# Two-layer chunked attention and retention trunk: value products a round later, column parts, later sines, side work spread by a running debt, logit scale inside the minimum

## The chip, the core and the metric

The kernel runs on one core of one Trainium2 chip. A core has a matrix engine (TensorE, PE in the profile; PEld is its weight load), a vector engine (VectorE, DVE), an activation engine (ScalarE, ACT), a general engine (GpSimd, POOL) and SyncE (SP), which here issues all DMA transfers. Each engine runs its own instructions in order and waits on semaphores for the others. The metric is the time of one execution on the device in microseconds. The kernel before took 2097.04 us, the median of 3 runs (2094.75 to 2097.13).

## The reference, cut to what matters

Two layers over 2048 tokens of width 1024. Each layer normalizes the rows, projects them to 4096 columns, runs softmax attention (8 heads of 64, own chunk of 64 and 8 chunks before, with a bias by distance) beside retention (4 heads of 128, a state carried from chunk to chunk), gates both and projects back.

```python
hn = rms_norm(x, norm_gain)
proj = hn @ w_in
aq, ak, av, ag, rq, rk, rv, rg = jnp.split(proj, cuts, axis=-1)
# attention, per head over its band of keys
scores = jnp.where(valid, einsum(qc, kb) * dh ** -0.5 + bias, NEG_INF)
ya = einsum(softmax(scores), vb)
# retention: q and k turned by cos, sin of the positions; decays per head
att = einsum(qc, kc) * intra_decay
o = einsum(att, vc) + einsum(qc * q_decay, state)
yr = rms_norm(o)
x = x + concat(ya * silu(ag), yr * silu(rg)) @ w_out
```

## The kernel before, in words

Each layer has 16 stages: four groups of heads `s` (two attention heads and one retention head each), and for each group four blocks `n` of 512 tokens. A stage is two generators: `dense_T` projects q, k and the retention's q, k with tokens along the columns (four accumulators, j = 0 to 3, 24 matmuls of 512 columns each), and `dense_V` projects values and gates for four token tiles (a = 0 to 3, 24 matmuls each). Every factor is split into an upper and a lower fp16 half (`hh`, `hl` for the rows, `g.h`, `g.l` for the weights), and three of the four cross products are summed, hence 24 matmuls for 8 slices of the inner dimension.

The order on PE, ACT, DVE and POOL is the order in which the program writes the instructions. It is woven by `run`: after each third of a dense product (a *round*, 8 matmuls) it calls `tick`, which writes the entries that `later(k, fn)` put off by k rounds; then one step of the attention of the stage before (`attention`, 8 units of three rounds: 4 token tiles `a` times 2 heads `hx`); then `pull`, which takes steps of the side work from the list `bg`. A stage has 24 rounds, 12 in each generator. Side work is: norms of later rows with the rotary tables (`norms_from_input`, `tables`, only in the first group of the first layer), the scaling and splitting of the next weights (`prep_T`, `prep_V`, `prep_O`), and at the end of a layer the first output rows (`wout_first`). How many steps a round takes is set in `run` from what is left, by rounding up:

```python
pull(min(-(-todo // max(left, 1)), todo))
```

An attention unit (`qk`, from L784) multiplies q by k into the one logit buffer `S` (L800, L801), adds the bias and takes the row maximum on DVE (L804), turns that into the exponent's offset on DVE (L806), takes exp on ACT (L807), rounds to fp16 on ACT (L809), forms the rest on POOL (L810), and lets SP transpose both halves by DMA into `pT` (L812). Two units later `flow(1)` calls `pv`: the value products on PE (L820 to L822), and a round after that the division by the row sum (L826, L827) and the gate (L832) on DVE. Before, `flow(1)` stands ahead of `qk` in the unit's first round. The buffers `sc` and `pq`, two of each, are shared with the rows of the output projection (`row_pair`).

PSUM holds two dense accumulators (`psD`), one logit buffer (`psS`) and a ring of four small tiles (`psR`) for value products, retention products (`decayed`, `retention`, L860) and column sums (`allsum`, L323). A dense accumulator comes free when DVE has taken the lower half from it: for q by L634, for k by L648, for a value tile by L766 to L770. In `dense_T` the evacuations of j = 0 and 1 (L631, L645) start the DMAs that lay out q and k; j = 2 and 3 are turned by the rotary tables (`swap`: halves swapped by DMA, three DVE operations L670, a split L673, L676). The very first stage works its first two accumulators in column parts of one token tile each (L712). Sines are taken in `tables` (L121, L122), on ACT, which for them loads another activation table. After the 16 stages `wout` projects back in 96 rounds (L1105) and forms the norms of the next layer.

Of the kernel before, what the change touches and what calls it, by code (L numbers as in the profile page):

```python
# [18 lines left out]
P = 128  # L19
# [8 lines left out]
def hybrid_trunk(ctx: ExitStack, tc: tile.TileContext, x, pos, gain, gcol, w_in, w_out, rel, fgain,  # L28
# [54 lines left out]
    def tables(n, wk):  # L83
# [35 lines left out]
        dve.tensor_scalar(k, k, HALF_PI, PI_CL, op0=ALU.add, op1=ALU.min)  # L119
        yield  # L120
        act.activation(r, ang, AF.Sin)  # L121
        act.activation(k2, k, AF.Sin)  # L122
# [12 lines left out]

    TAB_STEPS = 19

# [450 lines left out]
    def flow(k=0):  # L588

        if len(pipe) > k:  # L590
            pipe.pop(0)()
# [16 lines left out]
    def dense_T(l, s, n, g, st):  # L608
# [96 lines left out]
        if first:  # L705
# [72 lines left out]
    def attention(l, s, n, g, st, prev, nxt):  # L778
        units = []
        for a in range(4):  # L780
            for hx in range(2):
                units.append((a, hx))
        ya = {}

        def qk(a, hx):
# [10 lines left out]
            for j0, j1 in zip(cuts, cuts[1:]):  # L796
# [6 lines left out]
            m = b2.tile([P, 1], F32, tag="mq", name=f"mq{u.nm}")  # L803
            dve.tensor_tensor_reduce(out=v, in0=S[:, 0:w], in1=g.bias[hx][:, 640 - w:640], scale=1.0, scalar=-3.0e38,  # L804
                                     op0=ALU.add, op1=ALU.max, accum_out=m)
            dve.tensor_scalar(m, m, g.nc[:, 0:1], LN_PSC, op0=ALU.mult, op1=ALU.add)  # L806
            act.activation(v, v, AF.Exp, bias=m[:, 0:1], scale=g.c[:, 0:1])  # L807
            pq = b2.tile([P, 1280], F16, tag="pq", name=f"pq{u.nm}")
# [6 lines left out]
        def pv(u):  # L815
            t = 4 * n + u.a
            o = psR.tile([P, 512], F32, tag="small", name=f"o{u.nm}")
            for b, (q_, a_) in enumerate(u.kts):
                v_ = q_.v[:, a_, u.hx, :]
                pe.matmul(o[:, 0:65], u.p[:, b, :], v_[:, 0:65], start=(b == 0), stop=False)  # L820
                pe.matmul(o[:, 0:64], u.p[:, b, :], v_[:, 65:129], start=False, stop=False)  # L821
                pe.matmul(o[:, 0:65], u.p[:, u.nb + b, :], v_[:, 0:65], start=False, stop=(b == u.nb - 1))  # L822

            def out_():
                rl = b2.tile([P, 1], F32, tag="rl", name=f"rl{u.nm}")
                dve.reciprocal(rl, o[:, 64:65])  # L826
                dve.tensor_tensor(rl, rl, g.ka, op=ALU.mult)  # L827
                if u.hx == 0:
                    ya[u.a] = b2.tile([P, P], F32, tag="ya", name=f"ya{u.nm}")
                y = ya[u.a]  # L830
                vs = slice(u.hx * 64, u.hx * 64 + 64)
                dve.scalar_tensor_tensor(out=y[:, vs], in0=o[:, 0:64], scalar=rl[:, 0:1], in1=st.g[u.a][:, vs],  # L832
                                         op0=ALU.mult, op1=ALU.mult)
                if u.hx == 1:
                    sp.dma_start(y_d[t][:, s * P:(s + 1) * P], y)

            later(1, out_)

        ret = retention(l, s, n, g, st)
        for i, (a, hx) in enumerate(units):  # L840
            flow(1)
            u = qk(a, hx)
            yield
            if hx == 1:
# [307 lines left out]
    def run(gen, att, thirds):  # L1152
        left = thirds
        for _ in gen:
# [7 lines left out]
            if bg:  # L1162
                pull(min(-(-todo // max(left, 1)), todo))
            left -= 1
# [351 lines left out]
```

## Time and profile before

| | before |
|---|---|
| median of 3 runs | 2097.04 us |
| the profiled execution | 2094.75 us |
| its span, first to last instruction | 2092.8 us |
| PE busy | 2004.4 us (96%) |
| DVE, ACT, POOL busy | 1343.8, 1141.3, 432.9 us |
| mean granted PE clock | 0.991 |

A row of the waits gives engine, line, the releaser, then the total in us, the number of waits and the longest. A row of the timeline gives start, duration, engine, line, operation, output and inputs, shape and count, and in brackets the engine's idle time just before and who ended it. Overlapping durations of neighbouring matmuls come from pipelining; the distance between starts is what a matmul costs. A row of a stretch gives busy time and instructions of each engine, the granted clock, the DMA share and GB/s. The names are those of the program without buffer numbers: `dT`, `dV`, `dO` are the dense accumulators, `S` the logits, `o` the value product, `r` the retention products, `hTh` and `hTl` the halves of the normalized rows.

### The profile page before, as it was taken

How to read it: one execution, taken by the hardware profiler on the slowest of the kernel's cores; microseconds unless marked ns; L12 is line 12 of the kernel's file. 1: busy time of each engine (PE TensorE's matmuls, PEld its weight loads, DVE VectorE, ACT ScalarE, POOL GpSimd, SP SyncE). 2: the span in 40 equal slices, each digit the busy share in tenths (PEclk: the TensorE clock that was granted, in tenths of full speed). 3: DMA queues.
4: the chain of work that ended last, by engine and by line, in shares of the span. 5: the costliest groups of instructions: out<-in, count | busy, mean ns of one | idle time of the engine just before them, and what ended most of it. 6: DMA issues, size and time to landing. Idle time of an engine off the chain costs nothing.

```text
span 2092.8 us, 39599 instructions
## 1 busy us (share of the span) xinstructions
PE 2004.4 (96%) x14014; PEld 1049.4 (50%) x14014; DVE 1343.8 (64%) x4031; ACT 1141.3 (55%) x2522; POOL 432.9 (21%) x509
## 2 busy tenths in 40 slices
PE   6888999999999999998999999999999999998998
PEld 4344455555555555444444555555555555554443
DVE  7676666666656666576654666666666667656643
ACT  7455665556565654455444546554655565455432
POOL 1022222222122212121000222222222222222100
PEclk9999999999999999999999999999999999999999
DMA  8767674557476764599965556655655776558874
GB/s 247 171 127 162 136 166 114 115 112 159 110 169 133 161 166 99 113 211 260 219 185 113 120 102 142 130 121 106 155 123 118 178 156 162 117 100 183 212 199 123
DMA packets 645702, 313.65 MB, mean 150 GB/s; under 512 B 459232, under 2 KB 602080, under 8 KB 645504
## 3 DMA queue, kind: packets, MB, share of 16 engines
q1 hardware_dynamic: 645504, 311.12, 66.4%
q8 instruction: 110, 1.80, 0.4%
q14 instruction: 88, 0.72, 0.1%
HBM read 123.26 MB, written 41.98 MB: 79 GB/s over the span
## 4 chain that ended last, share of the span: by engine, by line
PE 55%; DMA 7%; DVE 5%; ACT 3%; issue 1%; SPq 1%; POOL 0%; POOLq 0%; DVEq 0%; ACTq 0%
PE dT L731 18%; PE dV L752 15%; PE dO L1105 12%; DMA pT<-pq 2%; PE r L860 2%; PE S L801 2%; PE S L800 2%; PE o L820 1%; PE o L821 1%; PE o L822 1%; DVE sc L804 1%; DMA swp<-rot 1%; DMA yhy<-rhy 1%; ACT sc L807 1%; ACT pq L809 1%
## 5 line engine op out<-in xcount | busy, mean ns | idle before, releaser
L810 POOL TENSOR_TENSOR pq<-sc,pq 128x640 f16<-128x640 f32 (+4 forms) x256 | 323.8, 1265 | 1175.9 <-issue 590.7
L807 ACT ACTIVATE sc<-sc,mq,cT 128x640 f32<-128x640 f32 (+4 forms) x256 | 218.5, 853 | 558.1 <-DVE mq L806 413.7
L752 PE MATMUL dV<-whV,hTh 128*128 128x512 f16 x1024 | 354.5, 382 | 13.0 <-DVE gt L770 12.8
L731 PE MATMUL dT<-hTh,whT 128*128 128x512 f16 x1008 | 349.4, 382 | 14.7 <-DMA hTh<-hTl 9.6
L752 PE MATMUL dV<-wlV,hTh 128*128 128x512 f16 x1024 | 354.1, 381 | 0.0
L752 PE MATMUL dV<-whV,hTl 128*128 128x512 f16 x1024 | 354.0, 381 | 0.0
L731 PE MATMUL dT<-hTl,whT 128*128 128x512 f16 x1008 | 346.6, 379 | 0.0
L731 PE MATMUL dT<-hTh,wlT 128*128 128x512 f16 x1008 | 346.6, 379 | 0.0
L752 PEld LDWEIGHTS <-hTh 128*128 128x128 f16 x2048 | 197.3, 98 | 227.7 <-DVE gt L770 16.4
L731 PEld LDWEIGHTS <-whT 128*128 128x128 f16 x2016 | 192.9, 98 | 221.6 <-issue 24.1
L804 DVE CUSTOM_DVE_ANT_0 sc<-S,bias 128x640 f32<-128x640 f32 (+4 forms) x256 | 188.4, 736 | 78.8 <-PE S L801 61.1
L1105 PE MATMUL dO<-whO,yly 128*128 128x512 f16 x512 | 194.1, 379 | 2.4 <-DMA yly<-rly 2.4
L1105 PE MATMUL dO<-whO,yhy 128*128 128x512 f16 x512 | 194.0, 379 | 1.2 <-DVE gt L770 0.6
L1105 PE MATMUL dO<-wlO,yhy 128*128 128x512 f16 x512 | 194.0, 379 | 0.0
L809 ACT ACTIVATE pq<-sc 128x640 f16<-128x640 f32 (+4 forms) x256 | 171.5, 670 | 10.9 <-DMA pT<-pq 3.0
L1105 PEld LDWEIGHTS <-yhy 128*128 128x128 f16 x1024 | 99.6, 98 | 115.1 <-issue 0.8
L752 PEld LDWEIGHTS <-hTl 128*128 128x128 f16 x1024 | 99.7, 98 | 105.0 <-issue 2.8
L800 PE MATMUL S<-k,q 128*128 128x128 f16 (+3 forms) x592 | 143.1, 268 | 7.9 <-DVE mq L804 7.9
L731 PEld LDWEIGHTS <-wlT 128*128 128x128 f16 x1008 | 97.2, 98 | 101.8 <-issue 1.1
L820 PE MATMUL o<-v,pT 128*128 128x65 f16 x1120 | 129.6, 193 | 10.2 <-DMA pT<-pq 9.7
L801 PE MATMUL S<-k,q 128*128 128x128 f16 (+3 forms) x592 | 130.5, 268 | 0.0
L820 PEld LDWEIGHTS <-pT 128*128 128x128 f16 x1120 | 105.3, 97 | 49.2 <-DMA pT<-pq 21.3
(350 smaller groups left out, 3352.7 us busy)
## 6 DMA issues: line engine op xcount, KB each, us to landing
q<-qq SPq DMA_DIRECT2D x128, 128.0 KB, 2.7
yyy<-y_d SPq DMA_DIRECT2D x32, 512.0 KB, 4.6
stT<-in_w_in_dram SPq DMA_DIRECT2D x27, 512.0 KB, 4.8
stV<-in_w_in_dram SPq DMA_DIRECT2D x26, 512.0 KB, 4.5
k<-kk SPq DMA_DIRECT2D x128, 64.0 KB, 2.0
swp<-rot SPq DMA_DIRECT2D x64, 128.0 KB, 2.5
tabc<-tab SPq DMA_DIRECT2D x32, 256.0 KB, 2.7
tabs<-tab SPq DMA_DIRECT2D x32, 256.0 KB, 2.9
```

Of the source, the lines that this page charges most:

```text
L731: pe.matmul(ps, w_[:, j, kt, :], h_[:, kt, :], start=(m == 0), stop=(m == 23))
L752: pe.matmul(ps, h_[:, kt, a * P:(a + 1) * P], w_[:, kt, :], start=(m == 0), stop=(m == 23))
L800: pe.matmul(o, st.q[:, hx, 0, cs], k_, start=True, stop=False)
L801: pe.matmul(o, st.q[:, hx, 1, cs], k_, start=False, stop=True)
L804: dve.tensor_tensor_reduce(out=v, in0=S[:, 0:w], in1=g.bias[hx][:, 640 - w:640], scale=1.0, scalar=-3.0e38, op0=ALU.add, op1=ALU.max, accu ...
L807: act.activation(v, v, AF.Exp, bias=m[:, 0:1], scale=g.c[:, 0:1])
L809: act.activation(pq[:, 0:w], v, AF.Copy)
L810: pool.tensor_tensor(pq[:, w:2 * w], v, pq[:, 0:w], op=ALU.subtract)
L820: pe.matmul(o[:, 0:65], u.p[:, b, :], v_[:, 0:65], start=(b == 0), stop=False)
L821: pe.matmul(o[:, 0:64], u.p[:, b, :], v_[:, 65:129], start=False, stop=False)
L860: pe.matmul(out_, w_, m_, start=(i == 0), stop=(i + 1 == len(pairs)))
L1105: pe.matmul(ps, h_[:, kt, :], w_[:, kt, :], start=(m == 0), stop=(m == 23))
```

## The change

Seven edits. (1) In `attention`, `flow(1)` is called after `qk` and the unit's first yield, a round later. (2) In the first group's stages n = 1, 2, 3, j = 0 and 1 of `dense_T` are worked in parts of 128 columns, in the order (0,0) (0,1) (0,2) (1,0) (1,1) (1,2) (0,3) (1,3), with a yield every 32 matmuls; both accumulators are evacuated in the sixth round. (3) In `tables` the sines come one step later, except in the first table. (4) `run` carries a fractional debt from round to round instead of rounding up. (5) The logits are scaled by -c on DVE as they are formed, with a minimum in place of the maximum; the constant is added on POOL; exp has the scale -1. (6) Both heads of a token tile share one PSUM tile and are divided by one reciprocal and one scalar product. (7) `TAB_STEPS` follows (3). The issuing of transfers in `qk`, `evacuate` and `swap` stands as it was.

```diff
+    lnp = cp.tile([P, 1], F32, tag="lnp", name="lnp")
+    pool.memset(lnp, LN_PSC)
...
         dve.tensor_scalar(k, k, HALF_PI, PI_CL, op0=ALU.add, op1=ALU.min)
         yield
+        if n:
+            yield
         act.activation(r, ang, AF.Sin)
         act.activation(k2, k, AF.Sin)
...
-    TAB_STEPS = 19
+    TAB_STEPS = 20
...
-        for j in range(2 if first else 0, 4):
+        parts = (l, s) == (0, 0) and n > 0
+        if parts:
+            ps, m = [None] * 2, 0
+            for (j, a) in ((0, 0), (0, 1), (0, 2), (1, 0), (1, 1), (1, 2), (0, 3), (1, 3)):
+                if a == 0:
+                    ps[j] = psD.tile([P, 512], F32, tag="dense", name=f"dT{nm}_{j}")
+                cs = slice(a * P, (a + 1) * P)
+                for i in range(24):
+                    w_, h_ = ((g.h, hh), (g.l, hh), (g.h, hl))[i // KT]
+                    pe.matmul(ps[j][:, cs], w_[:, j, i % KT, :], h_[:, i % KT, cs], start=(i == 0), stop=(i == 23))
+                    m += 1
+                    if m % 32 == 0 and m < 192:
+                        yield
+                if a == 3:
+                    evacuate(j, ps[j])
+            yield
+        for j in range(2 if first or parts else 0, 4):
...
-            dve.tensor_tensor_reduce(out=v, in0=S[:, 0:w], in1=g.bias[hx][:, 640 - w:640], scale=1.0, scalar=-3.0e38,
-                                     op0=ALU.add, op1=ALU.max, accum_out=m)
-            dve.tensor_scalar(m, m, g.nc[:, 0:1], LN_PSC, op0=ALU.mult, op1=ALU.add)
-            act.activation(v, v, AF.Exp, bias=m[:, 0:1], scale=g.c[:, 0:1])
+            dve.tensor_tensor_reduce(out=v, in0=S[:, 0:w], in1=g.bias[hx][:, 640 - w:640], scale=g.nc[:, 0:1],
+                                     scalar=3.0e38, op0=ALU.add, op1=ALU.min, accum_out=m)
+            pool.tensor_tensor(m, m, lnp, op=ALU.add)
+            act.activation(v, v, AF.Exp, bias=m[:, 0:1], scale=-1.0)
...
-            o = psR.tile([P, 512], F32, tag="small", name=f"o{u.nm}")
+            if u.hx == 0:
+                ring["o"] = psR.tile([P, 4, P], F32, tag="small", name=f"o{u.nm}")
+            o2 = ring["o"]
+            o = o2[:, u.hx]
...
+            if u.hx == 0:
+                return
 
             def out_():
-                rl = b2.tile([P, 1], F32, tag="rl", name=f"rl{u.nm}")
-                dve.reciprocal(rl, o[:, 64:65])
-                dve.tensor_tensor(rl, rl, g.ka, op=ALU.mult)
...
+                rl = b2.tile([P, 2], F32, tag="rl", name=f"rl{u.nm}")
+                dve.reciprocal(rl, o2[:, 0:2, 64])
+                dve.tensor_scalar(rl, rl, g.ka[:, 0:1], None, op0=ALU.mult)
+                y = b2.tile([P, P], F32, tag="ya", name=f"ya{u.nm}")
+                for hx in range(2):
+                    vs = slice(hx * 64, hx * 64 + 64)
+                    dve.scalar_tensor_tensor(out=y[:, vs], in0=o2[:, hx, 0:64], scalar=rl[:, hx:hx + 1],
+                                             in1=st.g[u.a][:, vs], op0=ALU.mult, op1=ALU.mult)
+                sp.dma_start(y_d[t][:, s * P:(s + 1) * P], y)
...
         for i, (a, hx) in enumerate(units):
+            u = qk(a, hx)
+            yield
             flow(1)
-            u = qk(a, hx)
-            yield
...
-        left = thirds
+        left, debt = thirds, 0.5
...
-                pull(min(-(-todo // max(left, 1)), todo))
+                debt += todo / max(left, 1)
+                pull(min(int(debt + 0.01), todo))
+                debt -= int(debt + 0.01)
```

More of the change, by code (lines that the diff above doesn't have):

```diff
@@ L782, in attention @@
                 units.append((a, hx))
-        ya = {}
         def qk(a, hx):
@@ L822, in pv @@
                 pe.matmul(o[:, 0:65], u.p[:, u.nb + b, :], v_[:, 0:65], start=False, stop=(b == u.nb - 1))
+            if u.hx == 0:
+                return
             def out_():
-                rl = b2.tile([P, 1], F32, tag="rl", name=f"rl{u.nm}")
-                dve.reciprocal(rl, o[:, 64:65])
[L827 to L835, printed above, removed]
+                rl = b2.tile([P, 2], F32, tag="rl", name=f"rl{u.nm}")
[7 more added lines that the diff above has]
+                sp.dma_start(y_d[t][:, s * P:(s + 1) * P], y)
             later(1, out_)
@@ L840, in attention @@
         for i, (a, hx) in enumerate(units):
-            flow(1)
             u = qk(a, hx)
             yield
+            flow(1)
             if hx == 1:
```

## The prediction

> **What bounds the kernel now.** First the head of the page, then PE's waits, longest first.
>
> ```profile
> span 2092.8 us, 39599 instructions
> ...
> PE 2004.4 (96%) x14014; PEld 1049.4 (50%) x14014; DVE 1343.8 (64%) x4031; ACT 1141.3 (55%) x2522; POOL 432.9 (21%) x509
> ```
>
> ```profile
> PE dV L752 <- DVE gt L770: 12.8, 6, 4.9
> PE o L820 <- DMA pT<-pq: 9.7, 11, 2.2
> PE dT L731 <- DMA hTh<-hTl: 9.6, 1, 9.6
> PE S L800 <- DVE mq L804: 7.9, 4, 3.3
> ...
> PE msT L323 <- DVE mbT L316: 3.3, 3, 1.9
> PE msV L323 <- DVE ya L832: 2.9, 2, 1.6
> PE dT L731 <- DMA hTh<-rhn: 2.8, 1, 2.8
> ...
> PE dT L731 <- issue: 2.2, 1, 2.2
> ```
>
> TensorE is the bound: it is idle for 2092.8 - 2004.4 = 88.4 us in all, and the change takes no work from it. So all that can be won lies in those 88.4 us and in a slower clock behind them. The stretches show where they lie.
>
> ```profile
> 100.00:130.00 30.00, 22.85 (x140) 11.08 (x138) 22.67 (x65) 17.82 (x38) 6.23 (x9) 0.99 0.65 126
> 300.00:500.00 200.00, 198.16 (x1485) 106.28 (x1485) 134.48 (x444) 115.48 (x272) 48.51 (x54) 1.00 0.58 122
> ...
> 192.50:196.00 3.50, 3.46 (x10) 1.26 (x10) 3.39 (x10) 1.16 (x3) 0.00 (x0) 0.50 0.41 95
> 204.90:208.50 3.60, 3.60 (x20) 1.53 (x21) 1.08 (x4) 1.37 (x5) 1.33 (x1) 0.57 0.81 156
> 878.10:881.50 3.40, 3.33 (x12) 1.59 (x12) 1.95 (x12) 3.02 (x6) 1.23 (x1) 0.50 0.20 39
> ```
>
> The columns are PE, PEld, DVE, ACT, POOL, granted clock, DMA share, GB/s. From 300 to 500 us PE is full (198.16 of 200): nothing is to be had in the steady part. The stages of the first section (50 to 260 us) and the layer ends (near 880 and 1890) have the holes, and behind each long hole some 3.4 us run at clock 0.50, a further 3.4 x 0.5 = 1.7 us. The holes one by one, from PE's timeline:
>
> ```profile
> 129.54 0.61 PE L752 MATMUL dV<-whV,hTh 128*128 128x512 f16 x1 [4.88 <-DVE gt L770]
> 192.54 0.61 PE L752 MATMUL dV<-whV,hTh 128*128 128x512 f16 x1 [4.25 <-DVE gt L770]
> 204.90 3.40 PE L731 MATMUL dT<-hTh,whT 128*128 128x512 f16 x8 [2.81 <-DMA hTh<-rhn]
> 878.17 0.27 PE L800 MATMUL S<-k,q 128*128 128x128 f16 x1 [3.28 <-DVE mq L804]
> 1891.00 0.27 PE L800 MATMUL S<-k,q 128*128 128x128 f16 x1 [3.18 <-DVE mq L804]
> ```
>
> Eight matmuls in 3.40 us after the hole of 2.81 are at half rate too (full rate is 0.22 us each, below). The Trainium skill (TensorE: Matmul & The Clock Gate, Part 1) puts the fall to half clock after an idle window of about 3.4 us; by that rule the holes of 2.81, 3.28 and 3.18 would cost only themselves, and about 5 us of my gain would not exist. The rows decide: half clock stands behind them.
>
> **Value products a round later.** One round is a third of a dense product: 8 matmuls and some attention work. The two last holes lie at the same place of the two layers, 1012.8 us apart, with 16 stages of 24 rounds and 96 rounds of the output projection between them: 2.1 us a round. The transposed probabilities are awaited 11 times, 9.7 us in all, the longest 2.2. A later product waits less by one round, unless the chain before it grows (POOL, below, about +0.4). 2.1 - 0.4 = 1.7 covers all but the tip of the longest ones: some -8. In the output projection some of it will only be waited for at the next transposed rows, so I take **-6**; bounds -9.7 and 0. S now stands ahead of the products on PE, which helps; nothing is queued between but the dense matmuls.
>
> **Side work spread evenly.** Same steps, same total; ends of runs flush the rest. Where 19 steps meet 12 rounds (last V stage of a layer), the old rule pulls 2 per round, the new 2,1,2,1,2. The hole at 878 comes from there:
>
> ```profile
> 877.29 0.82 DVE L804 CUSTOM_DVE_ANT_0 sc<-S,bias 128x640 f32<-128x640 f32 x1 [5.11 <-DMA yhy<-rhy]
> ```
>
> Unit 5's logits need the buffer "sc" in which output row 0 still waits for its transposes. Counting the pulls: before, row 0, then row 1 take the two buffers within rounds 2 and 3, ahead of unit 5 in round 4. After, row 1 comes in round 4 behind unit 5, which gets the other buffer. The wait for row 0's transposes passes from DVE to ACT (row 1's squares), some 5 us in which the gate evacuation of round 6 is late; its PSUM slot is needed in round 10, so that PE has 4 rounds, about 8 us, of cover. The two holes with their clock are 3.28 + 3.18 + 2 x 1.7 = 9.9; I take **-6**; bounds -9.9 and +2 (the ACT delay eating the cover). The waits of the column sums (3.3 + 2.9) shrink where two steps a round become 1.8: **-2**, bounds -6.2 and +2.
>
> **Column parts** in the three later stages of the first section. Their price is in the first stage, which already works so:
>
> ```profile
> 36.12 0.61 PE L712 MATMUL dT<-hTl,whT 128*128 128x128 f16 x8
> 36.57 0.61 PE L712 MATMUL dT<-hTh,wlT 128*128 128x128 f16 x8
> 37.01 0.38 PE L731 MATMUL dT<-hTh,whT 128*128 128x512 f16 x1
> 37.23 0.38 PE L731 MATMUL dT<-hTh,wlT 128*128 128x512 f16 x1
> ```
>
> 8 narrow ones start in 0.44 to 0.45 us, 56 ns each; a wide one takes 0.216. 192 narrow = 10.7 us against 48 wide = 10.4: +0.33 a stage, +1.0 in all. The gain: parts of three tiles can run before the fourth has landed. For stages 2 and 3 that can remove 2.2 + 2.81 + 1.7 = 6.7. For stage 1, the hole of 9.6, I expect nothing, because other things are late at the same place:
>
> ```profile
> 78.11 0.69 DVE L670 TENSOR_TENSOR raw<-raw,tabc 128x512 f32<-128x512 f32 x1 [7.20 <-DMA swp<-raw]
> ...
> 81.10 0.41 DVE L770 SCALAR_TENSOR_TENSOR gt<-gt,dV 128x256 f32<-128x256 f32 x1
> ...
> 85.30 0.68 DVE L676 TENSOR_TENSOR rot<-raw,rot 128x512 f16<-128x512 f32 x1
> ...
> 86.70 0.69 DVE L634 SCALAR_TENSOR_TENSOR qq<-dT,qq 128x512 f16<-128x512 f32 x1 [0.71 <-ACT qq L631]
> ...
> 91.77 0.60 ACT L645 ACTIVATE kk<-dT 128x512 f16<-128x512 f32 x1 [0.76 <-PE dT L731]
> ```
>
> The second dense PSUM slot is freed by L770 at 81.5, behind a DVE wait on the swapped halves; parts (0,0) to (0,2) can run from 70, then (1,0) waits until 81.5, and the retention product of round 3 until 86.0 (L676). From there 4 parts, 5.3 us, end near 91.5; before, the second accumulator is finished at 91.7 (L645's wait on PE). New loss: both accumulators now finish in one round, so the third one waits for the evacuation of the first (ACT 0.6, then L634 on DVE 0.7) with 1.3 us of PE work as cover instead of three rounds, and ACT may still be in exp and side work there, or, in stage 1, in the sines that now fall one round ahead of it: 0 to 3 a stage, I take 1.3 x 3 = 4. With +1.0 and 1 more in stage 1: -6.7 + 4 + 1 + 1 = about **-1**; bounds -7 and +8.
>
> **Later sines.** Two sines with a table load before and one after:
>
> ```profile
> 187.16 1.28 ACT L121 ACT_TABLE_LOAD   x1
> ...
> 189.28 0.26 ACT L760 ACTIVATE v<-dV 128x128 f16<-128x128 f32 x1
> 189.54 1.28 ACT L761 ACT_TABLE_LOAD   x1
> ```
>
> They stand right ahead of a value evacuation, and the holes of 4.88 and 4.25 (12.5 with clock) follow. Counting pulls: the sines move from V rounds 5 and 4 to V rounds 8 and 7. That is again ahead of an evacuation (round 9), so the table loads hold up the next one instead. And more norm steps fall into V (13 for 10) where DVE has 22.67 of 30 us. But the heap of side work ahead of the sines is thinner. **-3**; bounds -12.5 and +6.
>
> **Logit scale in the minimum.** DVE drops L806 and pays a pointer scalar in L804; POOL gets an add between L804 and exp.
>
> ```profile
> L925 DVE SCALAR_TENSOR_TENSOR yr<-r,rss,gt 128x128 f32<-128x128 f32 x128 | 44.4, 347 | 23.2 <-POOL rss L921 22.0
> L880 DVE TENSOR_TENSOR r<-r,msk 128x128 f32<-128x128 f32 x128 | 37.5, 293 | 6.3 <-PE r L860 6.3
> ```
>
> ```profile
> 129.40 0.27 DVE L210 TENSOR_SCALAR ssn<-ssn,gm,ge 128x1 f32<-128x1 f32 x1
> 129.74 0.55 POOL L212 TENSOR_TENSOR rsn<-ssn,mhalf 128x1 f32<-128x1 f32 x1 [6.53 <-DVE ssn L210]
> 130.71 0.21 DVE L806 TENSOR_SCALAR mq<-mq,ncT 128x1 f32<-128x1 f32 x1
> 131.01 0.81 ACT L807 ACTIVATE sc<-sc,mq,cT 128x512 f32<-128x512 f32 x1 [1.42 <-DVE mq L806]
> L827 DVE TENSOR_TENSOR rl<-rl,kaV x256: 159/159/1374, 99.4 to 1969.6; 128x1 f32<-128x1 f32 x128
> ```
>
> A pointer scalar adds about 347 - 293 = 54 ns; DVE gains 0.21 - 0.05. The chain to exp was 0.30 (L806's start to exp's start); through POOL it is 0.07 + 0.55 + 0.1 = 0.7, or less if an add is cheaper than the power: +0.4 a unit. ACT has 200 - 115.5 = 84 us idle in 200, so in the steady part it hides; in the loaded stages it makes every evacuation behind exp later: **+2**; bounds 0 and the rival below. Behind POOL's add queue only its own subtraction for the same unit and the powers, which follow exp anyway.
>
> **Both heads at once, clamp order.** One reciprocal and one product fewer per pair (two operations of L827's size, 0.16 us each at least, 128 times); DVE is not the bound: **0**, -1 where it is full. The PSUM tile is held three rounds longer, but one tile fewer is taken in six rounds, so the ring of four turns more slowly; were it short, a retention product would wait a round, 2.2.
>
> **Sum**: -6 - 6 - 2 - 1 - 3 + 2 = -16. The profiled execution took 2094.75 (span 2092.8 and 1.95 around it): 2078.8. The median shown is 2.3 above that execution, so 2081 for a median.
>
> **Rivals.** Narrow gain: products and layer ends pay (-12), but the third accumulator's wait costs its upper bound in all three stages (+8 instead of -1) and the sines give nothing: 2094.75 - 12 - 2 + 8 + 2 + 2.3 = 2093; if half, 2089. For it: L634 and the evacuation are serial; against: ACT's 30% idle there. Call it 2090.
> The change does not do what it says: the spread work lands in V, where DVE is already full, and the late products only uncover transposed output rows in the projection. Then only about -1 remains: 2096.
> Slower, one mechanism: POOL's add is held up by DVE. L827, as small an operation, takes 0.159 at best and 1.374 at worst, when a POOL subtraction runs beside it; the reverse holds for POOL's add if DVE's next instruction is one of the 1.28 us splits. Worst hop: 0.07 + 0.55 + 1.28 - 0.25 = 1.65 a unit. In the loaded stages (two V stages, two layer ends, 4 units each) ACT is what PE waits for: 16 x 1.65 = 26, less the -12 that products and ends keep: 2094.75 + 14 + 2.3 = 2111. It decides once the add usually ends over 1 us after L804. The Trainium skill (SBUF — State Buffer, SBUF: two separate sides) speaks for it: the port pair shared by the two engines is an exclusive lock held for a whole instruction; L827's spread agrees. Against it: in the steady part even 1.65 fits into ACT's 84 / 31 = 2.7 us idle per unit (three rounds, 6.3 us, a unit).
>
> **Chances.** Forecast 0.45 (2073 to 2088), a larger gain, with the sines' holes gone too, 0.05 (2068); narrow gain 0.17; no effect 0.15; slower 0.18. A change under 0.2%, 4.2 us, can't be told from none. Faster: 0.45 + 0.05 + 0.12 = 0.62; same: 0.05 + 0.12 = 0.17; slower: 0.03 + 0.18 = 0.21. The range leaves out the best case's end and the upper half of the slower one: 2067 to 2106.
>
> **What would show it.** Right: PE's wait for pT under 3 us; its wait for S behind L804 under 3; no hole for hTh at the start of stages 2 and 3; the hole of stage 1 split, its end unmoved near 91; a new wait of L731 on q's evacuation; L804 near 0.87 us; POOL's add under 0.6. Wrong: POOL adds over 1 us with exp later; the 4 to 5 us holes doubled rather than moved; PE clearly below 198 of 200 in the steady part, with which the whole sum falls.

## The result and the profile after

The changed kernel takes 2118.83 us, the median of 4 runs (2114.14 to 2122.85), against 2097.09 us before (4 runs, 2094.75 to 2097.94): a ratio of 1.0105, 95% interval 1.0082 to 1.0127. It is slower by about 22 us; the forecast was 2081, and its range ended at 2106. The profiled execution took 2114.14 us. The head of its page:

```profile
span 2112.3 us, 40180 instructions
...
PE 2014.1 (95%) x14446; PEld 1075.3 (51%) x14446; DVE 1270.2 (60%) x3519; ACT 1117.0 (53%) x2522; POOL 519.0 (25%) x766
```

Idle time of PE rose from 88.4 to 2112.3 - 2014.1 = 98.2 us, and its busy time by 10 us, to which more time at half clock belongs (the mean granted clock fell from 0.991 to 0.989). DVE has 74 us less to do, and that gained nothing. PE's waits after the change (line numbers have moved by some 20: L790 is the gate's evacuation that was L770, L823 the reduction that was L804, L825 the new add):

```profile
PE dT L731 <- DVE gt L790: 14.1, 5, 6.8
PE S L819 <- DVE mq L823: 11.3, 9, 3.4
PE dV L772 <- DVE gt L790: 8.9, 7, 4.4
PE r L882 <- DVE sh L890: 8.0, 7, 1.5
PE dT L751 <- DVE qq L638: 7.3, 3, 3.5
PE dO L1127 <- DVE gt L790: 6.3, 3, 2.6
...
PE o L842 <- DMA pT<-pq: 2.8, 1, 2.8
```

The wait for pT is gone (9.7 to 2.8), and so is every wait for hTh. But the logits S wait more (7.9 to 11.3), and other waits are new or far longer: dense products of q and k behind the gate's evacuation and the third accumulator behind q's evacuation (neither was there before), the retention product r behind its state sh (2.4 before), and the output projection behind the gate's evacuation (0.6 before). The main holes, from PE's timeline:

```profile
79.63 1.03 PE L731 MATMUL dT<-hTh,whT 128*128 128x128 f16 x8 [6.80 <-DVE gt L790]
...
129.82 0.39 PE L772 MATMUL dV<-whV,hTh 128*128 128x512 f16 x1 [4.44 <-DVE gt L790]
...
140.61 1.03 PE L731 MATMUL dT<-hTh,whT 128*128 128x128 f16 x8 [2.38 <-DVE gt L790]
...
162.35 0.38 PE L751 MATMUL dT<-hTh,whT 128*128 128x512 f16 x1 [2.73 <-DVE qq L638]
...
229.48 0.58 PE L751 MATMUL dT<-hTh,whT 128*128 128x512 f16 x1 [3.48 <-DVE qq L638]
...
509.98 0.22 PE L882 MATMUL r<-sh,rot 128*128 128x128 f16 x1 [1.05 <-DVE sh L890]
...
912.02 0.59 PE L1127 MATMUL dO<-whO,yhy 128*128 128x512 f16 x1 [2.59 <-DVE gt L790]
```

And two stretches, columns as before:

```profile
140.50:144.00 3.50, 3.39 (x33) 3.39 (x34) 2.38 (x6) 0.78 (x2) 0.19 (x1) 0.51 0.75 110
...
300.00:500.00 200.00, 196.25 (x1456) 105.04 (x1456) 127.89 (x383) 109.77 (x262) 58.09 (x85) 1.00 0.53 120
```

Even the steady part has fallen from 198.16 to 196.25 of 200. Where the time went can be read stage by stage. The table takes the start of each stage's first value matmul in PE's timeline, so that a stretch runs from one stage's value part to the next one's:

| stretch | before | after | loss |
|---|---|---|---|
| start to stage 1's value part | 103.6 | 102.6 | -1.0 |
| stage 1 to stage 2 | 62.5 | 72.8 | +10.3 |
| stage 2 to the second group | 126.0 | 127.6 | +1.6 |
| second group to layer 0's last stage | 567.5 | 570.9 | +3.4 |
| that to the output projection | 34.3 | 28.7 | -5.6 |
| first output projection, layer 1 to its last stage | 978.6 | 991.3 | +12.7 |
| that to the second projection | 34.2 | 28.8 | -5.5 |
| the rest | 186.2 | 189.6 | +3.5 |

Half of the span's 19.5 us is in one stretch, from stage 1 to stage 2 of the first section; the rest is spread in small steps, mostly about 1 us at a change of the group of heads and 3 to 4 us after the start of each projection. The two gains of some 5.5 are the holes for S near 880 and 1891, which did go.

### The profile page after: what moved, and what is told of

Same layout as the page of the kernel before. It is cut to its first block, busy times and chain, and to the rows that moved or that the text cites. A ratio compares the mean times of both kernels' runs of the same rounds, so it can differ in the third digit from the quotient of the medians.

```text
span 2112.3 us, 40180 instructions
## 1 busy us (share of the span) xinstructions
PE 2014.1 (95%) x14446; PEld 1075.3 (51%) x14446; DVE 1270.2 (60%) x3519; ACT 1117.0 (53%) x2522; POOL 519.0 (25%) x766
## 5 line engine op out<-in xcount | busy, mean ns | idle before, releaser
L826 ACT ACTIVATE sc<-sc,mq 128x640 f32<-128x640 f32 (+4 forms) x256 | 194.9, 761 | 567.4 <-POOL mq L825 567.0
L751 PE MATMUL dT<-hTh,whT 128*128 128x512 f16 x960 | 332.5, 380 | 7.3 <-DVE qq L638 7.3
L751 PE MATMUL dT<-hTh,wlT 128*128 128x512 f16 x960 | 332.4, 380 | 0.0
L751 PE MATMUL dT<-hTl,whT 128*128 128x512 f16 x960 | 332.3, 379 | 0.0
L772 PEld LDWEIGHTS <-hTh 128*128 128x128 f16 x2048 | 194.9, 98 | 212.7 <-DVE gt L790 12.2
L751 PEld LDWEIGHTS <-whT 128*128 128x128 f16 x1920 | 181.8, 98 | 181.4 <-issue 1.9
L825 POOL TENSOR_TENSOR mq<-mq,lnp 128x1 f32<-128x1 f32 x256 | 88.7, 346 | 702.6 <-DVE mq L823 614.2
L823 DVE CUSTOM_DVE_ANT_0 sc<-S,bias,ncT 128x640 f32<-128x640 f32 (+4 forms) x256 | 203.1, 793 | 37.8 <-PE S L820 29.4
L1127 PEld LDWEIGHTS <-yhy 128*128 128x128 f16 x1024 | 100.0, 98 | 123.1 <-issue 12.2
L819 PE MATMUL S<-k,q 128*128 128x128 f16 (+3 forms) x592 | 143.1, 268 | 11.3 <-DVE mq L823 11.3
L890 DVE SCALAR_TENSOR_TENSOR sh<-sh,state 128x128 f16<-128x128 f16 x120 | 92.5, 771 | 92.2 <-ACT sh L886 92.2
L751 PEld LDWEIGHTS <-wlT 128*128 128x128 f16 x960 | 92.6, 98 | 101.8 <-issue 9.3
```

What stands on the lines that cost most here:

```text
L751: pe.matmul(ps, w_[:, j, kt, :], h_[:, kt, :], start=(m == 0), stop=(m == 23))
L772: pe.matmul(ps, h_[:, kt, a * P:(a + 1) * P], w_[:, kt, :], start=(m == 0), stop=(m == 23))
L819: pe.matmul(o, st.q[:, hx, 0, cs], k_, start=True, stop=False)
L825: pool.tensor_tensor(m, m, lnp, op=ALU.add)
L826: act.activation(v, v, AF.Exp, bias=m[:, 0:1], scale=-1.0)
L890: dve.scalar_tensor_tensor(out=dst[:, 1], in0=dst[:, 0], scalar=-2.0 ** 11, in1=src, op0=ALU.mult, op1=ALU.add)
```

## The experiments

Effects in us below are ratios times 2094, the middle of before in most comparisons; 0.2% is 4 us. Each ratio is to the kernel before, measured beside it.

### One edit taken back at a time

My first theory was that the column parts and the spread of side work made the loss; the rival was the add on POOL. no_parts has the wide loop again, no_even the rounding up, no_pool_add the maximum with the scaling on DVE, no_late_pv `flow(1)` ahead of `qk`.

The hunks are those of the change's diff, taken back whole; for no_even:

```diff
-        left, debt = thirds, 0.5
+        left = thirds
...
-                debt += todo / max(left, 1)
-                pull(min(int(debt + 0.01), todo))
-                debt -= int(debt + 0.01)
+                pull(min(-(-todo // max(left, 1)), todo))
```

> The changed kernel with the column parts taken back (wide matmuls, one accumulator after the other, in stages 1 to 3 of the first section) and the other five edits kept. Theory 1 (column parts and the spread of side work are what costs): 2106 to 2111 us, 8 to 12 below the changed kernel; the stretch from the first value matmul of stage 1 to that of stage 2 is back from 72.8 to 62 to 65 us, and the wait of the third accumulator (L751) on q's evacuation (L638), 7.3 us, is gone. Theory 2 (the add on POOL between minimum and exp decides): within 3 us of the changed kernel, the stretch stays above 70. Theory 3 (the later sines moved the hole to the start of stage 2): gain of 0 to 4, and a hole of over 2 us behind the gate's evacuation (L790) remains in stage 2's first dense products.

> The changed kernel with the old rule for the side work (rounded up each round) and the other five edits kept. Theory 1: 2107 to 2112 us, some 9 below the changed kernel: the new 1 us holes at the six group changes, the later holes of the last retention product near 635 and 1655 and the 2.6 us holes at the starts of the output projections are gone; the hole near 880 and 1891 for S may come back with about 5 each, then only 2 to 4 are left of the gain. Theory 2 (POOL's add): within 3 us of the changed kernel.

> The changed kernel with the logit scale back behind a maximum (the scaling on DVE, no add on POOL) and the other five edits kept. Theory 1: within 3 us of the changed kernel's 2119. Theory 2 (the add on POOL decides): 2102 to 2108, some 15 below, and the waits for S behind L823 (11.3 us, 9 times) fall to under 5.

> The changed kernel with the value products a round earlier, as before the change, and the other five edits kept. If the later products do what was forecast, 2122 to 2127 us, 4 to 8 above the changed kernel, and the wait for the transposed probabilities is back from 2.8 to 8 us or more. If they are part of the loss (S ahead of the products on PE, and the heads' results later), at or below the changed kernel's 2119, and the waits for S behind L823 shrink from 11.3 us.

| | median, us | ratio | interval |
|---|---|---|---|
| the change | 2118.83 | 1.0105 | 1.0082 to 1.0127 |
| no_parts | 2126.57 | 1.0154 | 1.0135 to 1.0172 |
| no_even | 2105.05 | 1.0053 | 1.0035 to 1.0072 |
| no_pool_add | 2110.68 | 1.0077 | 1.0058 to 1.0096 |
| no_late_pv | 2121.77 | 1.0128 | 1.0108 to 1.0149 |

The expectation for no_parts failed in sign. Without the parts the kernel is slower by another 0.5%, and PE's timeline says why:

```profile
152.83 3.57 PE L735 MATMUL dT<-hTh,whT 128*128 128x512 f16 x8 [14.25 <-DMA hTh<-rhn]
...
226.36 3.57 PE L735 MATMUL dT<-hTh,whT 128*128 128x512 f16 x8 [12.62 <-issue]
```

At the starts of stages 2 and 3 the wide products wait 14.25 us for the normalized rows hTh and 12.62 us for something that the profile doesn't name ("issue"; the same rows are the likely one); before the change these two waits were 2.21 and 2.81. So some other edit makes the rows late, and the parts, which begin with three of the four tiles, hide most of it. The even spread costs 11 us and POOL's add about 6 (intervals overlap), both inside the changed kernel. That S would wait under 5 us without POOL's add did not come true: it waits 11.9. The later products are worth about 5 us there (intervals overlap); without them the wait for pT is 18.4 us instead of 2.8, as forecast for them.

### One edit alone, and the even spread with an earlier due

The new theory: rounding up did the side work early, and the even spread does the last steps late. add_even, add_sines and add_late_pv put one edit alone into the kernel before; pv_parts_heads puts in the later products, the parts and both heads at once.

> The kernel before with the even spread of side work alone. Revised theory 1: the old rule, rounding up in every round, does a run's side work early, so that the next group's normalised rows are transposed into hTh well ahead of its first dense product; spread evenly, the last steps fall into the last rounds of the run. Then hTh is late at the starts of stages 2 and 3 of the first section (wide products, so that all four tiles are waited for): 2104 to 2114 us, with a wait of L731 for hTh of 5 us or more that is 2.8 at most there before; and the one 1 us hole at each group change (retention product behind sh) appears. Theory 2 (the loss is made by the other edits): within 3 us of 2096.

> The kernel before with the later sines alone (one empty step more, 20 steps). Theory 1: the sines and the norm steps behind them come later, hTh a little: 2096 to 2102 us, the loss in the first section alone (up to 260 us). Theory 3 (the sines are the main cause): 2106 us or more. As the prediction had it: 2093.

> The kernel before with the value products a round later alone. As the prediction had it: about 2090 us (6 less), the wait for pT from 9.7 to under 3 us. If S ahead of the products only moves the waits: 2095 to 2099, with more waits for S behind L804 and for the retention rows.

> The kernel before with the later value products, the column parts and both heads at once; side work rounded up, sines and logit scale as before. Theory 1 (even spread, later sines and the add on POOL make the loss; parts are a gain of 3 to 7 since they wait for three of four tiles): 2083 to 2092 us, faster than both kernels. If the column parts cost by the wait of the third accumulator: 2096 or more, with that wait (L751 behind q's evacuation) of 5 us or more.

| | median, us | ratio | interval |
|---|---|---|---|
| add_even | 2127.21 | 1.0167 | 1.0148 to 1.0186 |
| add_sines | 2095.82 | 1.0018 | 1.0008 to 1.0028 |
| add_late_pv | 2098.35 | 1.0026 | 1.0015 to 1.0037 |
| pv_parts_heads | 2091.43 | 0.9990 | 0.9977 to 1.0003 |

The even spread alone costs 35 us, more than the whole change. The last transposes of the next rows on SP's queue, and what PE does then, before the change:

```profile
136.18 1.57 SPq L236 DMA_TRANSPOSE hTh<-rhn  x1
...
199.54 3.17 SPq L236 DMA_TRANSPOSE hTh<-rhn  x1
```

and with the even spread alone:

```profile
145.16 1.87 SPq L236 DMA_TRANSPOSE hTh<-rhn  x1
...
217.53 2.57 SPq L236 DMA_TRANSPOSE hTh<-rhn  x1
```

```profile
149.96 3.57 PE L731 MATMUL dT<-hTh,whT 128*128 128x512 f16 x8 [13.68 <-DMA hTh<-rhn]
...
222.27 3.57 PE L731 MATMUL dT<-hTh,whT 128*128 128x512 f16 x8 [11.82 <-issue]
```

The last transposes come 9 and 18 us later (12 of the 18 are the delay that stage 2 has already, its first value matmul at 178.3 instead of 166.0), and the first wide product of the stage starts 4.8 and 4.7 us behind their issue. even_due tells whether the lateness or the evenness costs: the same even spread, due some rounds earlier in these two stages.

```diff
                 if not first:
-                    run(dT, att, 10 if n == 0 else 14 if (l, s, n) == (0, 0, NS - 1) else 22 if (l, s) == (0, 0) else 24)
+                    run(dT, att, 10 if n == 0 else 14 if (l, s, n) == (0, 0, NS - 1) else 18 if (l, s) == (0, 0) else 24)
...
-                run(dense_V(l, s, n, g, st), att, 24 if n == NS - 1 and s < NSW - 1 else 12)
+                run(dense_V(l, s, n, g, st), att, 24 if n == NS - 1 and s < NSW - 1 else 9 if (l, s) == (0, 0) and 0 < n < NS - 1 else 12)
```

> The kernel before with the even spread alone, as in the run where only that was done (2127), but in stages 1 and 2 of the first section the side work is due earlier: 18 instead of 22 thirds from the start of the T part and 9 instead of 12 from the start of the V part, so that by count the last transposes of the next group's rows are issued in V round 9 instead of 12 (before the change: 10 and 9). Theory L (lateness of the last steps is what costs there, not how evenly they lie): the waits for hTh at the starts of stages 2 and 3 fall from 13.7 and 11.8 to 1 to 5 each, the stretch from stage 1's first value matmul to layer 0's second section is back by 12 to 17 us, and the time is 2110 to 2116. Theory S (evenly spread steps collide with evacuations wherever they lie): within 4 us of 2127.

It took 2104.65 us (1.0059, 1.0041 to 1.0078): 22 us less than add_even, a larger gain than theory L asked. Its transposes and the start of stage 2:

```profile
137.96 1.48 SPq L236 DMA_TRANSPOSE hTh<-rhn  x1
...
197.16 1.24 SPq L236 DMA_TRANSPOSE hTh<-rhn  x1
```

```profile
141.62 1.89 PE L731 MATMUL dT<-hTh,whT 128*128 128x512 f16 x8 [1.36 <-issue]
```

The wait is back at 1.36 us, and the second group starts at 288.7 us, where it started at 292.0 before the change: in this section lateness it is. What is left of the loss, 2102.8 - 2092.8 + 3.3 = 13 us by the spans, lies behind the first section. PE's waits in even_due from 288 us to the end:

```profile
PE o L820 <- DMA pT<-pq: 13.9, 12, 1.7
PE r L860 <- DVE sh L868: 7.9, 7, 1.5
```

Before the change the same two are 9.7 and 0.5 from there on, so they have grown by 4.2 + 7.4 = 12 us. That is not the whole: the even spread also shortens the two stretches ahead of the projections by 5.9 and 5.7 us here, so the other stretches lose about 25, and these two waits are about half of it. Where the second comes from can be read in the changed kernel, where ACT forms the next value weights at the change of a group:

```profile
504.07 0.29 ACT L886 ACTIVATE sh<-state 128x128 f16<-128x128 f32 x1
...
504.55 0.19 ACT L198 ACTIVATE urvV<-dcs 128x1 f32<-128x1 f32 x1
...
507.08 0.29 ACT L200 ACTIVATE raV<-raV,dcs 128x1 f32<-128x1 f32 x1
507.28 1.13 ACT L334 ACTIVATE whV<-stV,sV 128x1024 f16<-128x1024 f32 x1
```

```profile
508.44 1.28 DVE L337 SCALAR_TENSOR_TENSOR wlV<-stV,sV,whV 128x1024 f16<-128x1024 f32 x1 [1.01 <-ACT whV L334]
509.65 0.28 DVE L890 SCALAR_TENSOR_TENSOR sh<-sh,state 128x128 f16<-128x128 f16 x1
```

DVE's half of sh (L890) is queued behind the weights' split L337, which waited for ACT's L334, which stood behind eleven small operations; PE waits 1.05 us at 509.98. Before the change the same small operations ran from 491.46 to 493.98, ahead of sh, and PE had no hole there. That these steps fall a round later than before was read from the rows, not tested by itself; and why pT is waited for more was not followed further.

The later products alone cost 5 us where 6 of gain were expected. PE's waits in add_late_pv:

```profile
PE S L800 <- DVE mq L804: 13.0, 9, 5.3
...
PE r L860 <- DVE ya L832: 5.2, 6, 2.8
...
PE msT L323 <- DVE ya L832: 3.6, 6, 1.1
...
PE o L820 <- DMA pT<-pq: 2.7, 2, 2.4
```

pT is no longer waited for, as forecast, but two other waits have grown. S waits 5.1 us more, mostly at the layer ends; why wasn't followed. And the retention product r now waits for the gate ya, as the column sums msT do (3.6): o holds its small PSUM tile until ya has read it, and the ring of four is short once o comes a round later. Both heads at once take one tile fewer, and in pv_parts_heads the wait of r is not among the eleven longest, the last of which is 1.8 us. How much of the loss the ring makes was not measured by itself.

### The layer ends, the add, and the later products beside both heads

Here the base is pv_parts_heads (2091). even_ends adds the even spread in the last V stage of each layer alone; with_pool_add adds the logit scale in the minimum with POOL's add; parts_heads takes the later products out.

In even_ends `run` gets a flag, and the debt is used only where it is set:

```diff
-    run(dense_V(l, s, n, g, st), att, 24 if n == NS - 1 and s < NSW - 1 else 12)
+    run(dense_V(l, s, n, g, st), att, 24 if n == NS - 1 and s < NSW - 1 else 12,
+        (n, s) == (NS - 1, NSW - 1))
```

> The kernel with later products, column parts and both heads at once (2091), with the even spread added only in the last V stage of each layer (19 steps over 12 rounds). As the prediction had it for this place: 6 less, 2082 to 2087, with the holes for S near 880 and 1891 gone. If the last steps come late here too: the S holes go (about 5 each) but at the start of each output projection a wait behind the gate's evacuation of 2 us or more with a half clock behind it gives 3 to 4 of each back: 2086 to 2091.

> The same kernel (later products, column parts, both heads; 2091) with the logit scale in the minimum and the add on POOL. The prediction's own value is +2: 2091 to 2095. The prediction's slower rival (the add held up by DVE in the loaded stages): 2099 or more, the mean add there over 0.7 us. If the saving on DVE counts: 2087 to 2090.

> The kernel before with the column parts and both heads at once, the value products left where they were. Later products alone gave +5 us. If that loss holds beside the parts: 2084 to 2088, the fastest so far. If the loss came from the one-round shift of each head's division, which both heads at once takes back: 2091 to 2096, and the waits for pT are back at some 10 us.

even_ends: 2086.58 us (0.9969, 0.9959 to 0.9979), 4 us below its base and 0.3% below the kernel before. The holes for S are gone (stretch to the projection 27.9 and 28.1 instead of 34.8 and 34.7 us), but the second output weights are split in the last rounds, and the projection waits behind the gate's evacuation:

```profile
PE dO L1123 <- DVE gt L786: 7.5, 4, 2.7
PE S L815 <- DVE mq L819: 5.9, 8, 1.8
```

so that the first 96 matmuls of the two projections take 30.2 and 32.7 us instead of 27.0 and 27.5.

parts_heads: 2098.54 us (1.0034, 1.0022 to 1.0047), 9 us above pv_parts_heads, with the wait for pT at 11.3 us in 12 times. So the later products are worth 9 us beside both heads and the column parts, and cost 5 in the kernel before, which has neither.

with_pool_add: 2102.30 us (1.0049, 1.0032 to 1.0066), 12 us above its base. That is what the prediction's slower rival said of this edit. The add as a group, and its busy time in two stretches (one row each: loaded stages, steady part):

```profile
L823 POOL TENSOR_TENSOR mq<-mq,lnp 128x1 f32<-128x1 f32 x256 | 92.1, 360 | 685.7 <-DVE mq L821 589.9 <-DVE rl L848 24.3 <-DVE m2V L327 22.7
```

```profile
104.00:243.00 139.00, 10.22 (x16) 0.94 0.66 138
300.00:500.00 200.00, 10.55 (x32) 1.00 0.53 124
```

In the loaded stages an add takes 10.22 / 16 = 0.64 us, a little under the 0.7 expected for the rival, in the steady part 0.33. From the end of the reduction to the start of exp, without POOL's own record, it is 0.80 us on average in the loaded stages, 0.50 in the steady part; in pv_parts_heads 0.34 and 0.35. Two single ones on POOL and what DVE does beside the second:

```profile
138.68 0.19 POOL L823 TENSOR_TENSOR mq<-mq,lnp 128x1 f32<-128x1 f32 x1 [3.01 <-DVE rl L848]
...
187.69 1.10 POOL L823 TENSOR_TENSOR mq<-mq,lnp 128x1 f32<-128x1 f32 x1 [2.56 <-DVE mq L821]
```

```profile
187.53 0.08 DVE L821 DVE_READ_ACCUMULATOR2_ANT mq<- 128x1 f32 x1
187.53 1.22 DVE L233 TENSOR_TENSOR rln<-xin,rhn 128x1024 f16<-128x1024 f32 x1
```

Beside a reciprocal of two columns from PSUM the add takes 0.19 us, its least; when DVE's next instruction is a subtraction of two SBUF tiles of 1024 columns, the add ends where that one ends. The Trainium skill (SBUF — State Buffer, SBUF: two separate sides) names an exclusive lock of the port pair that the two engines share; 0.19 against 1.10 agrees with it.

### Add on DVE, rows early, with and without the column parts

dve_add is with_pool_add with the add alone moved:

```diff
-            pool.tensor_tensor(m, m, lnp, op=ALU.add)
+            dve.tensor_scalar(m, m, LN_PSC, None, op0=ALU.add)
```

even_ends_due is even_ends with the flag and even_due's dues in stages 1 and 2 as well (`norms` is `(l, s) == (0, 0) and 0 < n < NS - 1`):

```diff
-                run(dense_V(l, s, n, g, st), att, 24 if n == NS - 1 and s < NSW - 1 else 12,
-                    (n, s) == (NS - 1, NSW - 1))
+                run(dense_V(l, s, n, g, st), att,
+                    24 if n == NS - 1 and s < NSW - 1 else 9 if norms else 12,
+                    norms or (n, s) == (NS - 1, NSW - 1))
```

even_ends_due_wide is the same without the column parts; even_ends_due11 has 11 for the last 12, meant for the layer ends.

> The kernel with later products, column parts, both heads (2091) and the logit scale in the minimum, the constant added on DVE instead of POOL. Theory P (POOL's add is what costs the 11 us): 2089 to 2094, hop from the minimum to exp back at 0.33 us in the loaded stages. Theory D (the reduction with its pointer scalar and the changed order cost): 2099 to 2103 as with POOL's add.

> The kernel with later products, column parts, both heads and the even spread at the layer ends (2087), and in stages 1 and 2 of the first section the even spread too, due early (18 and 9 thirds). If early steps pay there beside the column parts: 2080 to 2085, with the stretch between the first value matmuls of stages 2 and 3 under 66 us (67.9 without). If the parts have already taken what there was: 2085 to 2090.

> As even_ends_due, without the column parts. Theory L (the parts only repair late rows): within 3 us of even_ends_due, no wait for hTh over 3 us at stages 2 and 3. If the parts pay by themselves: 5 us or more above it.

> The same, with the layer end's side work due after 11 thirds instead of 12. If the last steps, and not the order of the rows, make the wait behind the gate's evacuation at the start of the projection (2.7 us and a half clock): 2 to 5 below even_ends_due. If the rows' order goes back with it: the holes for S of about 5 a layer are back and it is 4 to 8 above.

| | median, us | ratio | interval |
|---|---|---|---|
| dve_add | 2089.74 | 0.9979 | 0.9968 to 0.9990 |
| even_ends_due | 2088.14 | 0.9980 | 0.9969 to 0.9990 |
| even_ends_due_wide | 2080.58 | 0.9938 | 0.9923 to 0.9953 |
| even_ends_due11 | 2107.68 | 1.0064 | 1.0049 to 1.0079 |

Theory P holds: with the same reduction, order and exp, and only the add back on DVE, the 12 us are gone, and from the reduction's end to exp it is 0.28 us in the loaded stages. The add as a group on DVE:

```profile
L823 DVE TENSOR_SCALAR mq<-mq 128x1 f32<-128x1 f32 x256 | 39.4, 154 | 8.9
```

even_ends_due met its second branch, no gain beside the parts. even_ends_due_wide missed both: with the rows early, the column parts do not merely stop paying, they cost 0.42%, 9 us. In even_ends_due the stretch from stage 1 to stage 2 is 69.6 us, without the parts 63.0. The row of the third accumulator with parts, then the row of the stage's start without them:

```profile
159.14 0.59 PE L747 MATMUL dT<-hTh,whT 128*128 128x512 f16 x1 [3.89 <-DVE qq L634]
```

```profile
139.85 1.89 PE L731 MATMUL dT<-hTh,whT 128*128 128x512 f16 x8 [1.11 <-issue]
```

A wait of 3.89 us for q's evacuation is bought with parts that would have saved 1.11. That is 2.8 of the 6.6 us; the rest is slower work, as the same stretch in both runs shows, first with parts, then without:

```profile
105.50:175.10 69.60, 56.90 (x501) 33.67 (x498) 49.15 (x129) 38.22 (x80) 14.98 (x19) 0.90 0.68 130
```

```profile
102.80:165.70 62.90, 54.07 (x355) 26.84 (x353) 47.19 (x125) 35.77 (x77) 14.36 (x18) 0.95 0.64 124
```

PE idles 69.60 - 56.90 = 12.7 us instead of 8.8, and its mean granted clock is 0.90 instead of 0.95, which is worth some 4 us by an estimate (0.10 x 69.6 - 0.05 x 62.9).

even_ends_due11's edit reached further than its expectation says: every V stage that had 12 thirds got 11, the two last ones among them. It shows that one third less for the same steps costs some 18 us over the whole kernel (1.0064 against 0.9980), with the value products' wait behind the gate's evacuation at 23.9 us instead of 11.3, and leaves the layer ends open. An earlier due is thus no gain in itself.

### Two last runs

best_mix is even_ends_due_wide with the minimum and dve_add's add; ends_due11 is even_ends_due_wide with

```diff
-                    24 if n == NS - 1 and s < NSW - 1 else 9 if norms else 12,
+                    24 if n == NS - 1 and s < NSW - 1 else 9 if norms else 11 if (n, s) == (NS - 1, NSW - 1) else 12,
```

> The fastest kernel so far (even_ends_due_wide, 2081) and the logit scale in the minimum with its constant added on DVE. Beside the column parts this pair was worth some 2 us: 2077 to 2081. If it is only the scatter of that kernel: 2079 to 2084.

> even_ends_due_wide (2081) with the side work of the last V stage of each layer alone due after 11 thirds instead of 12. If the last steps make the wait behind the gate's evacuation at the start of the projection: 2075 to 2079, that wait (7.5 us in 4) under 4. If the rows' order goes back with it: 2085 or more, the holes for S of about 5 a layer back.

best_mix: 2082.83 us (0.9941, 0.9927 to 0.9954), not to be told from even_ends_due_wide (0.9938): the minimum gains nothing there. ends_due11: 2086.70 us (0.9963, 0.9949 to 0.9977), 5 us worse. The stretch to the first projection grew from 28.1 to 31.8 us, with a new wait among its rows,

```profile
PE dV L752 <- DVE gt L770: 3.9, 1, 3.9
PE dO L1107 <- DVE gt L770: 2.2, 1, 2.2
```

while the S waits of 3.28 us near 880 did not return (the one left is 1.0): so neither branch of the expectation holds as it stands. Over the whole kernel the projection's wait behind the gate did fall below 4 (7.5 to 3.2), but the value products' wait behind the same evacuation rose from 12.2 to 19.6. The kernel even_ends_due_wide, 0.6% faster than before, stays the best of those run, with best_mix beside it.

## Why the prediction was wrong, point by point

Four of the runs build the change up step by step, and their ratios give each step its measured size beside the term of the sum:

| step | ratio from, to | measured, us | term of the sum, us |
|---|---|---|---|
| later products, column parts, both heads | 1, 0.9990 | -2 | -6 - 1 + 0 = -7 |
| logit scale, add on POOL | 0.9990, 1.0049 | +12 | +2 |
| later sines | 1.0049, 1.0053 | +1 | -3 |
| even spread, with its column sums | 1.0053, 1.0105 | +11 | -6 - 2 = -8 |

Forecast and measurement differ by 2119 - 2081 = 38 us; the four steps make 5, 10, 4 and 19 of them, so half of the miss is the even spread. The first and the third measured step are within the noise: the interval of pv_parts_heads reaches 1, and those of with_pool_add and no_even overlap.

**The step that failed: the even spread.** "Same steps, same total; ends of runs flush the rest" is true and was the error. The term was worked out at the layer ends alone, where it came out: the S holes went, 4 us net with even_ends. It left out when the last step of each run falls. With rounding up, a run of 21 steps in 22 thirds does one a round from the start and ends with rounds to spare; with the debt it ends in the last round by construction, and the last step is the transposes that the next stage's first matmul needs. I had counted these very pulls for the sines ("13 for 10" norm steps in V) and read the three more as load on DVE, not as rows that come later. By the same count the transposes' step moves from V round 10 to 12 in stage 1 and from 9 to 12 in stage 2; at 2.6 us a round (62.5 / 24, from stage 1 to stage 2 before) that is 5 and 8 us, and add_even shows 9 and 18 - 12 = 6. The bound of +2 was therefore no bound. even_due settles it for the first section of the kernel before: the same evenness with an earlier due takes 22 us back.

Inside the changed kernel the late rows cost less, since the parts hide most of them. From no_even to the changed kernel (spans 2101.6 and 2112.3) the first section, up to the second group's value part, loses 3 us, the two layer ends gain 11, and the other stretches lose 19: 4 in layer 0's groups, 12 from the first projection to layer 1's last stage, 3 after the second projection. In the changed kernel from 303 us on, r waits 5.3 us behind sh, and the projection 6.3 behind the gate's evacuation; in no_even from 300 us on the first of the two is not among the eleven longest and the second is 2.3. Here too the steps of the side work come later, but no run set an earlier due for them, so that this part of the cause is read from rows and not tested.

**The logit scale.** The mechanism was in the text, as the rival with 0.18, and right: POOL's add is held up by DVE's long instructions. Its threshold was wrong, "once the add usually ends over 1 us after L804". The add takes that long only beside the 1.22 and 1.28 us instructions, 0.64 on average in the loaded stages, and the edit cost 12 us all the same. The price of 16 units at 1.65 was too high, and the place was right in part: of the 11.7 us between the spans of pv_parts_heads and with_pool_add, 7.7 lie in the first section, most of the rest in the groups, and none in the layer ends, which the rival named too.

**The later products.** The wait for pT went as the term said. Alone the edit costs 5 us, beside both heads and the parts it gains 9. By the waits the sign hangs on an edit priced at nothing: the ring of four tiles, named in the last part ("were it short, a retention product would wait a round"), is short when the products come later and is relieved by both heads at once. No run has both heads without the parts in the kernel before, so that is not shown by itself.

**The column parts.** The wait on q's evacuation came in all three stages, 1.05, 2.73 and 3.48, within the bounds of 0 to 3 but for the last. Their value could not be read from the trace of before, since it hangs on how late the rows are: -10 in the changed kernel, +9 where the rows are early. That stage 1's third accumulator would not start earlier (90.96 against "near 91") was right.

**The later sines.** +4 alone (interval 2 to 6), within the bounds, not the -3: the hole of 4.44 us at 129.82 stayed, and a second one stands at 140.61.

Of the signs named in advance, three had come true for "wrong" in the trace of after: single adds over 1 us, the hole in stage 1's value part with a second one behind it instead of in its place, and a steady part below 198.

## What to carry to other kernels

When a pacing rule for background work changes, price the time of its last step, not only the load per round: list who waits for each run's last step and how many rounds it has moved, DMAs included. Moving everything earlier is no cure either: one round less for the same steps cost 18 us here. Two edits can each hide what the other breaks (parts and late rows; later products and both heads), so a sum of single terms is worth little until each is run alone or taken back alone. A small operation moved to an idle engine is not cheap if the busy one can hold it up and it stands in a chain.

## What the runs showed of the hardware

The smallest POOL add took 0.19 us, a third of the 0.55 of the power from which I had priced it, and 1.10 beside a DVE subtraction of two SBUF tiles: the price of that hop is set by the neighbour, not by the operation.

Behind a hole of 2.38 us PE ran at a granted clock of 0.51 for the next 3.5 us (the stretch from 140.50). Behind the longer hole of 2.73 us that ends at 162.35 the clock stayed full:

```profile
162.30:165.70 3.40, 3.35 (x20) 1.68 (x20) 3.20 (x7) 0.00 (x0) 0.00 (x0) 1.00 0.79 176
```

So the length of a hole alone did not decide whether it cost only itself. The Trainium skill (TensorE: Matmul & The Clock Gate, Part 1) puts the fall after an idle window of about 3.4 us; the fall behind 2.38 us does not agree with it, and the row decides.
